# A hybrid RWKV-7 and retention layer on one core: the doubling of the first two units 13 to 15 product groups later, the retention scores two groups later

## The chip, the cores and the metric

The kernel runs on one core of a Trainium2 chip. The metric is the device time of one execution in microseconds (us). Before the change the median of 3 runs is 1264.73 us (1264.21 to 1268.22).

## The reference, cut to what matters

One decoder layer on 256 tokens of width 2048. One input projection feeds two head groups. Group A is RWKV-7 time mixing (16 heads of 64, a state that is updated token by token), group B is retention (4 heads of 256). Their outputs are joined, go through one output projection, a layer norm, a squared-ReLU MLP of width 8192 and a second layer norm.

```python
def _hybrid_layer(x, ...):
    h = x @ w_in                                  # 2048 x 7424
    y_a = _rwkv7_mix(h[..., :RWKV_SHIFT_WIDTH], ...)
    q, k, v, g = jnp.split(h[..., RWKV_SHIFT_WIDTH:], RET_SPLITS, axis=-1)
    y_b = _retention_mix(q, k, v, g, ret_gn_w)
    mix = jnp.concatenate([y_a, y_b], axis=-1) @ w_o
    x = _layer_norm(ALPHA * x + mix, ln1_w, ln1_b)
    ff = jnp.square(jax.nn.relu(x @ w_up)) @ w_down
    return _layer_norm(ALPHA * x + ff, ln2_w, ln2_b)

def step(S, inp):                                 # RWKV-7, one token
    sa = jnp.einsum('bhvk,bhk->bhv', S, a_t)
    S = S * w_t[:, :, None, :] + sa[..., None] * b_t[:, :, None, :] + v_t[..., None] * k_t[:, :, None, :]
    y_t = jnp.einsum('bhvk,bhk->bhv', S, r_t)
```

## The kernel before, in words

**Large products.** All weights arrive as 202 chunks of 1 MB. A chunk comes as two halves `raw` (L138, on SP's queue), ScalarE rounds each half to `whi` (L140) and VectorE takes the rest `wlo = raw - whi` (L141), so that three float32r products stand for one float32 product. `whi` and `wlo` have four buffers each, `raw` three. TensorE then runs the chunk: 48 products of 256 columns in `stat_tile` (L157), or 24 of 512 columns in `mov_chunk` (L173). A quarter of a chunk is a **group**: 12 products of 256 columns, or 6 of 512. After each group the generator yields. The input projection has 58 chunks, so 232 groups.

**Small work between the groups.** `large()` (L506) runs the large products in a fixed order: the low-rank inputs, then for u = 0 to 3 the k, r and v columns of RWKV unit u (4 heads, a quarter of group A), and after each a share of the retention (`RET_SPLIT`). `interleave` (L840) calls, after each group, every live `rwkv_unit(u)` whose count has run down. `yield LAG["x"]` in a unit means: go on after so many groups. One unit runs through these steps:

- the decay and the norm of k (L558 to L617), which end in `kk`, `bt`, `ar` (L624 to L631);
- `gram` (L644): four blocks of 64 x 64 products with `ar`, masked by VectorE (L646);
- the inverse of a unit triangular 32 x 32 block for all heads at once, 31 pairs of a product `prod` (L699) and a sum into `xb` (L701) on VectorE;
- the **round trip**: `xb` goes to DRAM (`dxt`, L708) and comes back as `xc` in another layout (L710), on SP's queue, where the loads of `raw` also stand;
- the second head sum and the bonus (`head_sum`, L583 and L584; L730 to L732), then `xt`, the transposed `xc` (L736), then `yield LAG["bg"]`, which is 4;
- the **doubling**: the inverse of the 64 x 64 block from those of the two 32 x 32 blocks, `d1` (L747) and `d2` (L758) on TensorE with copies `pt` (L751) and `xt` (L763) between;
- the **state steps**, four of them (L770 to L817), each with `f1` (L779, L781), a copy `rhs` by ScalarE (L784), a product (L787), a copy `sa` (L789), `f2` (L795, L796), the new state on VectorE (L803 to L806) and `f3` (L810 to L813); lags of 2, 2 and 1 groups stand between them;
- the head norm and the result into `mxh` and `mxl` (L820 to L838).

The retention counts in groups too: `later(RLAG[0], ...)` (L478) runs the scores of a head (L420, L422) four groups after its rotated `qk` have been set going on POOL (L471, L472), and `later(RLAG[1], ...)` runs `outputs` (L432 to L445) four groups after those. The gate (L487 to L503) reads what `outputs` leaves in `vt`.

**The order on each engine.** The text above is only the program's order. A scheduling layer then lays out each engine's queue: it may put an instruction that it takes to be ready ahead of one that it takes to be still waiting. Within a queue nothing overtakes. So a lag sets where a step may stand, not where it does. Small tiles in PSUM (`sm`) share four banks.

The line that the change replaces, and the two tables:

```python
LAG = dict(..., vtok=8, bg=4, d1=3, d2=1, f1=1, sa=2, st=2, yc=2)   # L81
RLAG = (4, 4)                                                       # L83
            xt = tmp("xt")
            V.transpose(out=xt, in_=xc)
            yield LAG["bg"]                                         # L737
```

Of the kernel before, what the change touches and what calls it, by code (L numbers as in the profile page):

```python
# [77 lines left out]

STRETCH = (78, 106, 138, 170)

LAG = dict(lora=2, scan=3, sq=5, rn=1, kk=7, bt=2, g1=1, btok=1, ktok=2, g2=1, sub=3, xt=2, vtok=8, bg=4, d1=3, d2=1, f1=1, sa=2, st=2, yc=2)  # L81

RLAG = (4, 4)  # L83

SUB_YIELD = (6, 10, 13, 16, 19, 21, 23, 25, 27, 29)
NSHORT = 10
# [15 lines left out]
def tile_hybrid_layer(ctx, tc, xT, xtok, ws, pp, lup, glup, ln1r, ln2r, cst, rope, dmask, eye, out):  # L102
# [14 lines left out]
    def sm_bank():  # L117
        return ps.tile([P, 512], F32, name="sm", tag="sm", bufs=4)
# [115 lines left out]
    def dcol(base, j):  # L234
        return dp[:, base + j:base + j + 1]
# [38 lines left out]
    with ExitStack() as rctx:  # L274
# [7 lines left out]
        def tmp(name, bufs=1, n=512):  # L282
            if name in LONG or n < 256:
                return rp.tile([P, n], F32, name=name, tag=name, bufs=2 if name in TWO else bufs)
            if name in RET:
                return rp.tile([P, n], F32, name=name, tag="rshort", bufs=4)
            return rp.tile([P, n], F32, name=name, tag="short", bufs=NSHORT)
# [112 lines left out]
        def retention():  # L400
# [4 lines left out]
            def later(n, fn):  # L405
                pend.append([n, fn])
# [10 lines left out]
            def scores(h, vt, q, k, dmt):  # L417
                sc = sm_bank()
                for i in range(2):
                    TE.matmul(sc[:, 0:T], k[:, T * i:T * i + P], q[:, hs[i]], start=i == 0, stop=i == 1)  # L420
                for i in range(2):
                    TE.matmul(sc[:, T:T + P], k[:, T * i + P:T * i + T], q[:, T * i + P:T * i + T],  # L422
                              start=i == 0, stop=i == 1)
                pm = tmp("pm", n=384)
                V.tensor_tensor(out=pm[:, 0:T], in0=sc[:, 0:T], in1=dmt, op=ALU.mult)
                V.tensor_tensor(out=pm[:, T:T + P], in0=sc[:, T:T + P], in1=dmt[:, 0:P], op=ALU.mult)
                later(RLAG[1], lambda: outputs(h, vt, pm))

            def outputs(h, vt, pm):
                yb = sm_bank()  # L430
                hv = slice(T * (h % 2), T * (h % 2) + T)
                TE.matmul(yb[:, 0:T], pm[:, 0:P], vt[:, 0, hv], start=True, stop=True)  # L432
                TE.matmul(yb[:, T:2 * T], pm[:, P:T], vt[:, 0, hv], start=True, stop=False)
                TE.matmul(yb[:, T:2 * T], pm[:, T:T + P], vt[:, 1, hv], start=False, stop=True)
                st6 = tmp("st6", n=12)
                mv = tmp("mv", n=4)
                for tt in range(2):
                    V.bn_stats(out=st6[:, 6 * tt:6 * tt + 6], in_=yb[:, hs[tt]])
                    V.bn_aggr(out=mv[:, 2 * tt:2 * tt + 2], in_=st6[:, 6 * tt:6 * tt + 6])
                var = tmp("rvar", n=2)  # L440
                V.tensor_scalar(out=var, in0=mv.rearrange("q (a b) -> q a b", b=2)[:, :, 1], scalar1=RET_EPS,
                                scalar2=None, op0=ALU.add)
                rs = rsqrt(rp, var, 2)
                for tt in range(2):
                    V.tensor_scalar(out=vt[:, tt, hv], in0=yb[:, hs[tt]], scalar1=mv[:, 2 * tt:2 * tt + 1],  # L445
                                    scalar2=rs[:, tt:tt + 1], op0=ALU.subtract, op1=ALU.mult)

            for n in range(2):
# [9 lines left out]
                for h in (2 * n, 2 * n + 1):  # L458
# [18 lines left out]
                    nc.gpsimd.dma_start(out=dmt, in_=dmask[:, T * h:T * h + T])  # L477
                    later(RLAG[0], lambda h=h, vt=vt, qk=qk, dmt=dmt: scores(h, vt, *qk, dmt))  # L478
                    yield "end"
# [43 lines left out]
        def rwkv_unit(u):  # L523
# [16 lines left out]
            def split(src):  # L540
                t = rp.tile([P, 512], F32R, name="lsp", tag="short", bufs=NSHORT)
                hi, lo = t[:, 0:T], t[:, T:2 * T]
                S.copy(hi, src)
                V.tensor_tensor(out=lo, in0=src, in1=hi.bitcast(F32), op=ALU.subtract)
                return hi, lo
# [6 lines left out]
            lus = split(lupt)  # L552
            yield LAG["lora"]
            pw, pa = sm_bank(), sm_bank()
# [3 lines left out]
            for p, j in enumerate(js):  # L558
                S.activation(s[:, hs[p]], pw[:, hs[p]], AF.Tanh, bias=dcol(W0H, j), scale=0.5)
                S.activation(a[:, hs[p]], pa[:, hs[p]], AF.Tanh, bias=dcol(A0H, j), scale=0.5)  # L560
            yield LAG["scan"]
            V.tensor_scalar(out=s, in0=s, scalar1=0.5, scalar2=0.5, op0=ALU.mult, op1=ALU.add)
# [12 lines left out]
            def head_sum(src, lag):  # L575
# [4 lines left out]
                V.tensor_tensor(out=lo, in0=src, in1=hi.bitcast(F32), op=ALU.subtract)  # L580
                yield LAG[lag]
                bank = sm_bank()
# [7 lines left out]
            kkr, sq = tmp("kkr"), tmp("sq")  # L590
            for p, j in enumerate(js):
# [8 lines left out]
                            op0=ALU.mult, op1=ALU.add)  # L600
            yield LAG["rn"]
            S.activation(t, y, AF.Square)
            G.tensor_tensor(out=t, in0=t, in1=v, op=ALU.mult)
            yield LAG["rn"]
            V.scalar_tensor_tensor(out=t, in0=t, scalar=10.0 / 3, in1=t, op0=ALU.subtract, op1=ALU.mult)
            V.scalar_tensor_tensor(out=y, in0=t, scalar=5.0, in1=y, op0=ALU.add, op1=ALU.mult)
            S.activation(t, y, AF.Square)
            yield LAG["rn"]
            V.scalar_tensor_tensor(out=t, in0=t, scalar=9.0 / 64, in1=v, op0=ALU.mult, op1=ALU.mult)
            V.scalar_tensor_tensor(out=y, in0=t, scalar=3.0, in1=y, op0=ALU.subtract, op1=ALU.mult)  # L610
            kk = kkr
# [15 lines left out]
            bt, kt_ = tmp("bt"), tmp("kt")  # L627
# [8 lines left out]
            g1, g2 = tmp("g1", n=1024), tmp("g2", n=1024)  # L636
# [28 lines left out]
            def tok(src, name):  # L665

                t, w = tmp(name), tmp("sw")[:, 0:256].rearrange("q (g x) -> q g x", x=32)
                V.transpose(out=t, in_=src)
                for h in range(2):
                    up, dn = slice(64 * h, 64 * h + 32), slice(64 * h + 32, 64 * h + 64)  # L670
                    if name in TOK_V:
                        V.transpose(out=v8(t)[up, :, 32:64], in_=v8(src)[dn, :, 0:32])
                        V.transpose(out=v8(t)[dn, :, 0:32], in_=v8(src)[up, :, 32:64])
                    else:
                        S.copy(w[dn], v8(t)[up, :, 32:64])
                        S.copy(v8(t)[up, :, 32:64], v8(t)[dn, :, 0:32])
                        S.copy(v8(t)[dn, :, 0:32], w[dn])
                return t
# [7 lines left out]
            btok = tok(bt, "btok")  # L686
# [4 lines left out]
            ktok = tok(kt_, "ktok")  # L691
# [28 lines left out]
            vtok = tok(v, "vtok")  # L720
# [5 lines left out]
            g, gg, bg = tmp("g"), tmp("gg"), tmp("bg")  # L726
# [7 lines left out]
            done["free", "v", u] = True  # L734
            xt = tmp("xt")
            V.transpose(out=xt, in_=xc)  # L736
            yield LAG["bg"]  # L737


            def c32(p, n):  # L740
# [27 lines left out]
            st = None  # L768
            for n in range(4):
# [18 lines left out]
                sa = tmp("sa", n=128)  # L788
# [26 lines left out]
                if n < 3:  # L815
                    st = sn
# [6 lines left out]
            yc, ysq = tmp("yc"), tmp("ysq")  # L823
# [17 lines left out]
        def interleave(main, units):  # L841
# [12 lines left out]
            for e in live:  # L854
                for _ in e[1]:
                    pass

        interleave(large(), [rwkv_unit(u) for u in range(4)])


# [325 lines left out]
```

## Time and profile before

| | value |
|---|---|
| median of 3 runs | 1264.73 us (1264.21 to 1268.22) |
| profiled execution, its own time | 1258.88 us |
| span of that execution | 1257.1 us |
| TensorE busy | 1217.3 us, 97% of the span |
| VectorE busy | 840.7 us, 67% |
| ScalarE busy | 560.3 us, 45% |
| GpSimd busy | 101.6 us, 8% |
| DMA | 229.76 MB, 183 GB/s over the span |
| share of the chain that ended last | TensorE 78%, VectorE 9%, DMA 5%, ScalarE 3% |

TensorE's share counts an instruction from its start to its modelled end, and products overlap in the array, so an engine that is "busy" may still be far from its pace. The pace is read from how many products stand in a stretch. The input projection with the units takes the first 470 us or so; after it come the output projection, the MLP and the two norms.

### The profile page before, as it was taken

How to read it: one execution, taken by the hardware profiler on the slowest of the kernel's cores; microseconds unless marked ns; L12 is line 12 of the kernel's file. 1: busy time of each engine (PE TensorE's matmuls, PEld its weight loads, DVE VectorE, ACT ScalarE, POOL GpSimd, SP SyncE). 2: the span in 40 equal slices, each digit the busy share in tenths (PEclk: the TensorE clock that was granted, in tenths of full speed). 3: DMA queues.
4: the chain of work that ended last, by engine and by line, in shares of the span. 5: the costliest groups of instructions: out<-in, count | busy, mean ns of one | idle time of the engine just before them, and what ended most of it. 6: DMA issues, size and time to landing. Idle time of an engine off the chain costs nothing.

```text
span 1257.1 us, 21910 instructions
## 1 busy us (share of the span) xinstructions
PE 1217.3 (97%) x8952; PEld 1096.0 (87%) x8952; DVE 840.7 (67%) x1319; ACT 560.3 (45%) x723; POOL 101.6 (8%) x89
## 2 busy tenths in 40 slices
PE   7998998999999999989999999999999999999996
PEld 7988997879999778769988899988999888999885
DVE  6888897889879855786554555545555545555566
ACT  5545345355435433464444444443444434444341
POOL 0102121001101100008200000000000000000001
PEclk9999999999999999999999999999999999999998
DMA  8565355346444537655655655555555555556553
GB/s 284 201 190 167 96 181 166 86 139 206 141 140 162 172 111 254 196 169 211 240 200 192 206 191 190 187 199 193 198 195 193 193 193 199 191 190 198 186 200 102
DMA packets 86185, 229.76 MB, mean 183 GB/s; under 512 B 30530, under 2 KB 30658, under 8 KB 85316
## 3 DMA queue, kind: packets, MB, share of 16 engines
q1 hardware_dynamic: 83924, 219.38, 53.4%
q0 software_dynamic: 1440, 7.87, 1.8%
q8 instruction: 70, 1.15, 0.4%
q10 hardware_dynamic: 720, 1.11, 0.3%
q14 instruction: 31, 0.25, 0.1%
HBM read 224.59 MB, written 3.74 MB: 182 GB/s over the span
## 4 chain that ended last, share of the span: by engine, by line
PE 78%; DVE 9%; DMA 5%; ACT 3%; issue 1%; POOL 0%; DVEq 0%; ACTq 0%; SPq 0%
PE mm L157 34%; PE mm L173 34%; DMA raw<-in_ws_dram 4%; PE mm L193 3%; DVE wlo L141 3%; PE sm L644 1%; ACT whi L140 1%; DVE prod L699 1%; DVE xb L701 1%; DMA xc<-dxt 1%; DVE wx L141 1%; PE sm L787 1%; PE sm L779 0%; PE sm L810 0%; ACT wx L140 0%
## 5 line engine op out<-in xcount | busy, mean ns | idle before, releaser
L141 DVE TENSOR_TENSOR wlo<-raw,whi 128x1024 fp32r<-128x1024 f32 x372 | 464.1, 1249 | 315.7 <-ACT whi L140 309.0
L140 ACT CAST whi<-raw 128x1024 fp32r<-128x1024 f32 x372 | 391.2, 1052 | 534.7 <-PE mm L157 217.1
L157 PE MATMUL mm<-x1l,whi 128*128 128x256 f32 x928 | 257.1, 277 | 0.0
L157 PE MATMUL mm<-x1h,whi 128*128 128x256 f32 x928 | 257.1, 277 | 0.0
L157 PE MATMUL mm<-x1h,wlo 128*128 128x256 f32 x928 | 257.1, 277 | 0.0
L157 PE MATMUL mm<-xh,whi 128*128 128x256 f32 x640 | 181.4, 283 | 0.0
L157 PE MATMUL mm<-xl,whi 128*128 128x256 f32 x640 | 178.8, 279 | 0.0
L157 PE MATMUL mm<-xh,wlo 128*128 128x256 f32 x640 | 178.1, 278 | 0.0
L157 PEld LDWEIGHTS mm<-x1l,whi 128*128 128x128 f32 x928 | 175.0, 189 | 0.0
L173 PE MATMUL mm<-whi,ul 128*128 128x512 f32 x448 | 174.3, 389 | 0.0
L173 PE MATMUL mm<-whi,uh 128*128 128x512 f32 x448 | 174.3, 389 | 0.0
L173 PE MATMUL mm<-wlo,uh 128*128 128x512 f32 x448 | 174.3, 389 | 0.0
L157 PEld LDWEIGHTS mm<-x1h,wlo 128*128 128x128 f32 x928 | 174.2, 188 | 0.0
L157 PEld LDWEIGHTS mm<-x1h,whi 128*128 128x128 f32 x928 | 174.2, 188 | 0.0
L157 PEld LDWEIGHTS mm<-xh,whi 128*128 128x128 f32 x640 | 120.8, 189 | 3.2 <-issue 1.0
L157 PEld LDWEIGHTS mm<-xl,whi 128*128 128x128 f32 x640 | 120.7, 189 | 1.1 <-issue 0.2
L157 PEld LDWEIGHTS mm<-xh,wlo 128*128 128x128 f32 x640 | 120.7, 189 | 0.3
L173 PEld LDWEIGHTS mm<-wlo,uh 128*128 128x128 f32 x448 | 84.1, 188 | 17.6
L173 PEld LDWEIGHTS mm<-whi,ul 128*128 128x128 f32 x448 | 84.1, 188 | 17.5
L173 PEld LDWEIGHTS mm<-whi,uh 128*128 128x128 f32 x448 | 84.1, 188 | 17.1
L173 PE MATMUL mm<-whi,xh 128*128 128x512 f32 x128 | 51.9, 406 | 0.0
L1076 POOL TENSOR_TENSOR z<-z,lnr 128x512 f32<-128x512 f32 x3 | 3.9, 1293 | 593.6 <-DVE stats L1064 593.6
(272 smaller groups left out, 1621.6 us busy)
## 6 DMA issues: line engine op xcount, KB each, us to landing
raw<-in_ws_dram SPq DMA_DIRECT2D x400, 512.0 KB, 4.4
first<-in_ws_dram SPq DMA_DIRECT2D x8, 256.0 KB, 7.5
z<-in_xtok_dram POOLq DMA_DIRECT2D x2, 1024.0 KB, 11.3
lnr<-in_ln1r_dram POOLq DMA_DIRECT2D x2, 1024.0 KB, 5.4
lnr<-in_ln2r_dram POOLq DMA_DIRECT2D x2, 1024.0 KB, 11.5
xraw<-in_xT_dram SPq DMA_DIRECT2D x3, 512.0 KB, 8.3
dn<-g SPq DMA_DIRECT2D x8, 128.0 KB, 3.8
xc<-dxt SPq DMA_DIRECT2D x8, 128.0 KB, 3.5
```

Of the source, the lines that this page charges most:

```text
L140: S.copy(hi, raw)
L141: V.tensor_tensor(out=lo, in0=raw, in1=hi.bitcast(F32), op=ALU.subtract)
L157: TE.matmul(dst, w[:, c], a, start=n == 0, stop=n == 3 * KT - 1)
L173: TE.matmul(dsts[tt], a, w[:, c], start=first and k4 == 0 and j == 0, stop=last and k4 == 3 and j == 2)
L193: TE.matmul(dst, a, wt[:, o:o + w], start=kq == 0 and k4 == 0 and i == 0, stop=kq == 3 and k4 == 3 and i == 2)
L644: TE.matmul(bank[r, 128 * n:128 * n + 128], src[r, c64(p, n)], ar[r, o:o + 128], start=True, stop=True)
L699: V.tensor_tensor(out=pv, in0=xbv[0:q, 8 - m:8, s0 + 1:32], in1=blkv[0:q, s0:s0 + 1, s0 + 1:32].broadcast_to([q, m, t]), op=ALU.mult)
L701: V.tensor_reduce(out=xbv[0:q, 8 - m:8, s0], in_=pv, axis=AX.X, op=ALU.add)
L787: both(lambda r, p, cp: TE.matmul(sb[r, cp], xt[r, c64(p, n)], rhs[r, cp], start=True, stop=True))
L1076: G.tensor_tensor(out=z[:, tt, cb(n)], in0=z[:, tt, cb(n)], in1=lnr2[:, 0, cb(n)], op=ALU.mult)
```

## The change

The wait after `xt` no longer has one length for all units. It becomes 19 groups for unit 0, 17 for unit 1, and stays 4 for units 2 and 3. The retention scores come six groups after the rotation instead of four. Nothing is computed in another way.

```diff
-LAG = dict(lora=2, scan=3, sq=5, rn=1, kk=7, bt=2, g1=1, btok=1, ktok=2, g2=1, sub=3, xt=2, vtok=8, bg=4, d1=3, d2=1, f1=1, sa=2, st=2, yc=2)
-
-RLAG = (4, 4)
+LAG = dict(lora=2, scan=3, sq=5, rn=1, kk=7, bt=2, g1=1, btok=1, ktok=2, g2=1, sub=3, xt=2, vtok=8, d1=3, d2=1, f1=1, sa=2, st=2, yc=2)
+
+RLAG = (6, 4)
+
+BGLAG = (19, 17, 4, 4)
...
             V.transpose(out=xt, in_=xc)
-            yield LAG["bg"]
+            yield BGLAG[u]
```

From here on the changed kernel's lines have numbers that are higher by two. The queues as built show what the table does to the order.

**TensorE, the doubling of unit 0 and what follows it.** L747 is `d1`, L758 `d2`, L779 `f1` and L787 the product after it, all of unit 0; L583 and L584 are the first head sum of unit 1 and L157 the large products. Before:

```order
L157 MATMUL mm<-xh,wlo 128x256
L747 MATMUL sm<-xc,g_747 32x32
L583 MATMUL sm<-hi,ones 128x512
L584 MATMUL sm<-lo,ones 128x512
L157 MATMUL mm<-xh,whi 128x256
...
L747 MATMUL sm<-xc,g_747 32x32 x15
...
L758 MATMUL sm<-xt,pt 32x32
L779 MATMUL sm<-vtok,g_748 64x64 x3
...
L787 MATMUL sm<-rhs,xt 64x64
```

Now (L749 is `d1`, L760 `d2`, L781 `f1`, L789 the product after it; L646 is the gram of unit 1):

```order
L749 MATMUL sm<-xc,g_747 32x32 x16
L646 MATMUL sm<-ar,bt 64x128 x8
...
L646 MATMUL sm<-ar,kt 64x128 x8
...
L760 MATMUL sm<-xt,pt 32x32 x16
...
L781 MATMUL sm<-vtok,g_748 64x64 x4
...
L789 MATMUL sm<-rhs,xt 64x64 x4
```

Counted in groups of large products from the start, the first `d1` of unit 0 stood behind 73.0 groups and the other fifteen behind 73.8; now all stand behind 75.0. The head sum of unit 1, which stood behind the first `d1` at 73.0, now stands alone at 62.0. The state steps of unit 0 stood in 74.2 to 82.0 and now stand in 79.0 to 97.0. Unit 1 goes the same way: its `d1` from 117.8 to 121.0, its state steps from 118.9 to 130.0 into 125.0 to 143.0. The state steps of unit 2 stand in 172.0 to 190.0 in both. From its `d1` (168.0) on the queue is as before, save for the scores, two groups later (204 to 206 and 220 to 222 for the last two heads).

**VectorE, the same place.** L141 (now L143) takes the low half of a weight, L699 and L701 (L701 and L703) are the inverse of unit 0, L596 to L612 (L598 to L614) the norm of k in unit 1, L736 (L738) the transposition of `xc` for unit 0. Before:

```order
L701 TENSOR_REDUCE xb<-prod 32x8
L631 TENSOR_TENSOR ar<-r,dc 128x8x64
L141 TENSOR_TENSOR wlo<-raw,whi 128x1024 x3
L596 TENSOR_SCALAR v<-sm 128x512
L736 STREAM_TRANSPOSE xt<-xc 128x512
L597 TENSOR_SCALAR t<-v 128x512
L599 TENSOR_SCALAR y<-t 128x512
L680 TENSOR_TENSOR k<-k,kf 128x512
L763 COPY xt<-sm 32x8x32 x2
L141 TENSOR_TENSOR wlo<-raw,whi 128x1024
```

Now:

```order
L703 TENSOR_REDUCE xb<-prod 32x8
...
L612 SCALAR_TENSOR_TENSOR y<-t,y 128x512
L143 TENSOR_TENSOR wlo<-raw,whi 128x1024
L614 SCALAR_TENSOR_TENSOR kkr<-y,kkr 128x512
L143 TENSOR_TENSOR wlo<-raw,whi 128x1024 x2
L628 TENSOR_TENSOR ar<-kkr,s 128x8x64
L630 TENSOR_TENSOR a<-a,kkr 128x512
L633 TENSOR_TENSOR ar<-r,dc 128x8x64
L631 TENSOR_TENSOR bt<-a,di 128x512
...
L143 TENSOR_TENSOR wlo<-raw,whi 128x1024
L738 STREAM_TRANSPOSE xt<-xc 128x512
```

The norm of k of unit 1 stood behind the transposition of `xc`; now it is mixed into the inverse of unit 0 and done before it. The last sum into `xb` stood behind 33 low halves and now stands behind 31; the transposition stood behind 36 and now stands behind 35.

## Rows read from the trace of the kernel before

**Rows 1.** Page, part 1: span, and busy time of each engine.

```profile
span 1257.1 us, 21910 instructions
PE 1217.3 (97%) x8952; PEld 1096.0 (87%) x8952; DVE 840.7 (67%) x1319; ACT 560.3 (45%) x723; POOL 101.6 (8%) x89
```

**Rows 2.** Busy time in stretches: length, each engine's busy us (count), clock, DMA.

```profile
98.00:118.00 20.00, 19.50 (x167) 19.14 (x168) 19.02 (x40) 11.65 (x16) 2.80 (x3) 1.00 0.52 167
118.00:157.00 39.00, 36.78 (x516) 33.45 (x515) 31.73 (x58) 12.01 (x21) 6.70 (x6) 1.00 0.41 113
211.00:258.00 47.00, 42.82 (x526) 37.52 (x526) 34.36 (x65) 13.25 (x23) 6.55 (x6) 0.93 0.43 125
312.00:366.00 54.00, 54.00 (x652) 49.28 (x652) 41.38 (x72) 21.40 (x34) 6.08 (x6) 1.00 0.48 149
```

**Rows 3.** The same stretches, products of 256 columns (L157) alone: PE, PEld.

```profile
118.00:157.00 39.00, 22.28 (x162) 19.45 (x161) 1.00 0.41 113
211.00:258.00 47.00, 22.40 (x151) 19.41 (x150) 0.93 0.43 125
312.00:366.00 54.00, 34.71 (x274) 32.31 (x274) 1.00 0.48 149
```

**Rows 4.** The same stretches, products of 512 columns (L173) alone.

```profile
118.00:157.00 39.00, 0.00 (x0) 0.00 (x0) 1.00 0.41 113
211.00:258.00 47.00, 5.05 (x21) 3.85 (x22) 0.93 0.43 125
312.00:366.00 54.00, 6.35 (x24) 4.27 (x24) 1.00 0.48 149
```

**Rows 5.** Chain that ended last: start us, length us, what.

```profile
118.49 4.28 DMA dxt<-xb
122.78 2.75 DMA xc<-dxt
...
195.43 16.24 PE mm L157 x144
211.67 6.62 DMA xc<-dxt
...
260.33 5.50 PE mm L173 x24
```

**Rows 6.** Timeline around both round trips: start us, length us, instruction, idle before.

```profile
118.07 0.39 DVE L701 TENSOR_REDUCE xb<-prod 32x8 f32<-32x248 f32 x1
...
125.57 0.24 PE L747 MATMUL sm<-xc,g 32*32 32x32 f32 x2 [2.22 <-DMA xc<-dxt]
...
206.43 0.40 DVE L701 TENSOR_REDUCE xb<-prod 32x8 f32<-32x248 f32 x1
...
213.87 0.28 PE L157 MATMUL mm<-xh,wlo 128*128 128x256 f32 x1
...
218.33 0.31 PE L747 MATMUL sm<-xc,g 32*32 32x32 f32 x2 [4.18 <-DMA xc<-dxt]
...
219.59 0.41 PE L157 MATMUL mm<-xh,whi 128*128 128x256 f32 x1
219.83 0.69 DVE L596 TENSOR_SCALAR v<-sm 128x512 f32<-128x512 f32 x1 [3.62 <-PE sm L584]
```

**Rows 7.** Waits: who waited for whom, us in total, times, longest.

```profile
PE sm L420 <- POOL qk L472: 3.9, 3, 1.9
...
PE sm L493 <- issue: 1.3, 1, 1.3
...
PE sm L583 <- ACT hi L579: 1.4, 1, 1.4
```

**Rows 8.** VectorE by line and form from 98 to 158 us: count, busy us, mean ns.

```profile
L805 DVE TENSOR_TENSOR st<-sm,st 128x64 f32<-128x64 f32 x4 | 0.7, 220 | 0.2
...
L609 DVE SCALAR_TENSOR_TENSOR t<-t,v 128x512 f32<-128x512 f32 x1 | 0.7, 692 | 0.5 <-ACT t L607 0.5
...
L599 DVE TENSOR_SCALAR y<-t 128x512 int32<-128x512 int32 x1 | 0.4, 427 | 0.0
```

**Rows 9.** Page, part 5: the split on VectorE over the whole span.

```profile
L141 DVE TENSOR_TENSOR wlo<-raw,whi 128x1024 fp32r<-128x1024 f32 x372 | 464.1, 1249 | 315.7 <-ACT whi L140 309.0
```

## The prediction

> **What bounds the kernel now.** I read the page's busy shares first, then the busy time by stretch, then the chain and the timeline at the two places where TensorE stands still. TensorE counts as busy for 97% of the span [rows 1], so whatever the change can gain must lie in how slowly it goes while it is "busy". For that the pace has to be known. In the chain 144 products of 256 columns take 16.24 us and 24 of 512 columns 5.50 us [rows 5]: 0.113 and 0.229 us each where nothing disturbs. A group, 12 of the one or 6 of the other, is thus 1.36 to 1.37 us.
>
> The reader should now take three stretches [rows 2] in which the small work is the same: one unit's doubling and state steps, the next unit's gram, one head sum. From 118 to 157 us (unit 0 with the gram of unit 1) there are 162 products of 256 columns [rows 3]: 39.0 - 162 x 0.113 = 20.7 us go to everything else. From 211 to 258 us (unit 1 with the gram of unit 2) there are 151, and 21 of 512 columns [rows 3, 4]: 47.0 - 17.1 - 4.8 = 25.1 us. From 312 to 366 us (unit 2 with the gram of unit 3) there are 274 and 24: 54.0 - 31.0 - 5.5 = 17.5 us. The same small work costs 3.2 us more at unit 0 and 7.6 us more at unit 1 than at unit 2.
>
> The timeline says why. At unit 0 the last sum into `xb` begins at 118.07 us and `d1` starts at 125.57, after 2.22 us in which TensorE stood [rows 6]; between them lie the two transfers, 4.28 and 2.75 us [rows 5]. At unit 1 it is 206.43 to 218.33 us with 4.18 us of standing, and the second transfer alone takes 6.62 us. After that wait a product of 256 columns is shown with 0.41 us [rows 6], and the mean granted clock of the stretch is 0.93 [rows 2]: some 6.6 of the 47 us were at the lower of the two levels, 1.2 GHz. And the state steps, which a lag should set apart, had piled up behind the late `d1`: 8 groups at unit 0 instead of the 18 that they span at unit 2. With few large products between two steps, TensorE waits for each copy.
>
> **The change, part by part.** (a) The doubling. In the order as built `d1` itself moves little (73.8 to 75.0 groups, 117.8 to 121.0). What changes is what stands around it. The head sum of unit 1 no longer stands behind the waiting `d1` but 11 groups earlier, and the state steps spread over 18 groups, step for step as they stand at unit 2 in the kernel before. So I price both places by unit 2: -3.2 and -7.6, together **-10.8 us**. This holds the two standing waits (2.2 + 4.2), the time at the lower clock, and the piled-up steps. The other end is 0, if the same steps wait as long where they now stand.
>
> (b) The scores. TensorE stands for 3.9 us in three waits on POOL's `qk`, the longest 1.9 us [rows 7]. Two groups are 2.7 us, more than any of them. POOL's queue itself moves only at the first head, where a small load slips between the two rotations. I take **-3.0 us**; the ends are -3.9 and 0. `outputs` of the first head of all moves behind 123 groups, but its result is read only by the gate at 144.
>
> (c) VectorE's front. The norm of k of unit 1, some eight instructions with three that follow it, comes forward into the inverse of unit 0: nine at 0.69 and two at 0.4 us [rows 8], 7.0 us of work ahead of four to six splits. There VectorE has no room: 19.02 of 20 us busy from 98 to 118 us [rows 2]. A split is 1.25 us [rows 9] and serves 24 products, 2.7 us of TensorE; with four buffers VectorE may be 4 x 2.7 = 10.8 us ahead. If that lead is full, 7 us fit into it and the cost is 0; if it is empty, the whole 7 us are paid. Just before, TensorE already waited 1.4 us behind a late rounding for a head sum [rows 7], so the lead isn't always there. I take **+3.0 us**, between 0 and 7. The work is paid back from 118 us on, where VectorE is busy for only 31.7 of 39 us.
>
> (d) VectorE's own wait for `xc`. From the last sum into `xb` to `d1` it took 7.5 and 11.9 us [rows 6]. In the new order four splits and some six instructions of 0.7 us lie between that sum and the transposition of `xc`, about 9 us: the transposition comes 0 to 3 us too early. The row shows what such a wait is like: VectorE stood 3.62 us before L596 and did no split meanwhile [rows 6]. The Trainium skill ("TensorE: Matmul & The Clock Gate", section "Architectural detail: the array is 16× 32×32, not 1× 128×128") speaks against the change here: it calls VectorE's queue strict FIFO, so a transposition that waits holds every split behind it. By that rule alone what TensorE no longer waits for would be waited for by VectorE, (d) would be +6.5 and the sum -4.3 us; the 3.62 us agree that such waits happen. By the rows I take +0.5, since the lead of (c) hides part, and another +0.5 for the gate of the first retention half, where TensorE now waits 1.3 us [rows 7] and the head norm of unit 1 now falls into the same groups: **+1.0 us**, between 0 and 6.
>
> What costs nothing: unit 0 ends some 15 groups later, and its result is read by the second half of unit 1, which moves by only 3 groups, and by the output projection, behind 232. From `d1` of unit 2 the queues are as before. If that cover were gone, the last unit's tail would follow the last large product and every step would be bare; the order shows that it isn't. The later scores of the last head leave 6 groups, 8 us, between its `outputs` (now 226) and the gate (232).
>
> Sum: -10.8 - 3.0 + 3.0 + 1.0 = **-9.8 us**. The profiled execution took 1258.88 us around a span of 1257.1, so it would take 1249.1; it lies 5.9 us below the median of the runs. I put the same difference on the median: 1264.73 - 9.8 = **1255 us**. The best ends of all terms give -14.7, and with the late head sum of 1.4 and the gate's 1.3 us gone as well -17.4: 1247 us.
>
> **The rivals.** *The wait moves to VectorE.* The transposition waits for `xc` by 3 us at each unit, splits come late, and (c) costs its 3: -10.8 - 3.0 + 3.0 + 6.0 + 0.5 = -4.3, 1260.4 us. For it: the in-order wait of 3.62 us [rows 6] and the round trip of 11.9 us at unit 1. Against it: at unit 0 it was 7.5 us, less than the work between.
>
> *The piling is not what costs.* If the steps wait as long wherever they stand, because VectorE and ScalarE are full with the inverse of unit 1, which now runs beside the state steps of unit 0, only the two standing waits go: -6.4, and +4.0 from (c) and (d), with no gain from the scores: -2.4, 1262.3 us. At unit 2 no inverse ran beside the steps; VectorE was busy for 41.4 of 54 us there [rows 2]. That is what this rival has for it. This is also the case in which the change doesn't do what it says.
>
> *VectorE becomes the bound: slower.* If VectorE enters the front without a lead, (c) costs 7, and then each of the three new states of units 0 and 1 (four instructions of 0.2 us [rows 8]) is found behind one split and two inverse steps, 1.25 + 0.8 = 2 us, while `f1` stands two groups on in TensorE's queue: 6 x 2 = 12. Then -10.8 - 3.0 + 7 + 12 = +5.2, 1269.9 us. It decides where the lead, 10.8 us at most, is used up before the state steps begin. Against it: over the four stretches together VectorE is busy for 126.5 of 160 us [rows 2], so a lead that is lost comes back.
>
> **How the numbers follow.** My forecast has 0.66, the first rival 0.16, the second 0.10, the third 0.08. A measurement of this kernel tells about 0.3%, 3.8 us, from no change. The forecast's own range, -17 to -5, is wholly beyond that; the first rival lies at its edge and counts half; the second is within it. Faster 0.74, same 0.18, slower 0.08. The range from 1246 to 1263 us holds the forecast, the first rival and the middle of the second.
>
> **What would show it.** Right: no wait of TensorE for `xc` over 0.5 us; no stretch at the lower clock near unit 1; the same account (stretch minus products at their pace) near 17.5 us over each of the two new stretches of state steps; the wait of L420 on POOL below 1 us. Wrong: VectorE's transposition of `xc` idle for 3 us or more, or large products that wait for `wlo` between 98 and 150 us, or new waits of L781 for the state on VectorE.

## The result, and the profile after

The changed kernel takes 1248.97 us in the median of 4 runs (1243.16 to 1252.39) against 1264.47 us for the kernel before, measured beside it (1263.71 to 1268.22, 4 runs): a ratio of 0.989, 95% interval 0.985 to 0.9936, some 15.5 us faster. Its profiled execution took 1243.16 us around a span of 1241.4; that of before took 1258.88.

The first two lines of its page, and the shares by engine of the chain that ended last (the page's fourth part):

```profile
span 1241.4 us, 21909 instructions
...
PE 1209.7 (97%) x8952; PEld 1089.2 (88%) x8952; DVE 845.8 (68%) x1319; ACT 559.8 (45%) x723; POOL 102.7 (8%) x89
...
PE 85%; DVE 5%; ACT 2%; DMA 2%; issue 1%; POOL 0%; DVEq 0%; SPq 0%; ACTq 0%
```

TensorE's busy share is 97% as before [rows 1], which by itself tells nothing. The chain does: TensorE's share of it rose from 78% to 85%, and VectorE and DMA, 9% and 5% before, fell to 5% and 2%. What the chain no longer holds is seen in TensorE's waits from 50 to 480 us (us in total, times, longest):

```profile
PE sm L585 <- ACT hi L581: 3.2, 2, 2.0
PE sm L646 <- DVE bt L631: 1.7, 2, 1.4
PE sm L646 <- DVE kt L683: 1.0, 1, 1.0
PE mm L175 <- DVE mxl L840: 0.5, 1, 0.5
PE mm L159 <- DVE wlo L143: 0.5, 1, 0.5
PE sm L495 <- DVE gth L492: 0.4, 1, 0.4
PE sm L586 <- DVE lo L582: 0.2, 1, 0.2
```

The waits for `xc`, 2.2 and 4.2 us [rows 6], are gone, and so are the three on POOL's `qk`, 3.9 us [rows 7]; the gate's 1.3 us fell to 0.4. The same view of the kernel before has these two lines:

```profile
PE sm L583 <- ACT hi L579: 2.6, 2, 1.4
PE sm L644 <- DVE bt L629: 0.4, 1, 0.4
```

So the gram's waits for `bt` and `kt` grew from 0.4 to 2.7 us, and those of the head sums for `hi` from 2.6 to 3.2. Both are for results of the front of VectorE and ScalarE, which now holds more. A wait of 0.5 us of a large product for `wlo` is new as well.

Three stretches of the changed kernel in which the doubling and the state steps of units 0, 1 and 2 stand, first all work, then the products of 256 columns (L159), then those of 512 (L175); columns as in [rows 2]:

```profile
125.00:178.00 53.00, 52.02 (x650) 48.19 (x649) 49.22 (x115) 18.29 (x27) 7.93 (x8) 1.00 0.55 165
216.00:269.00 53.00, 51.56 (x549) 42.30 (x547) 50.37 (x147) 15.91 (x25) 2.98 (x3) 1.00 0.44 133
303.00:357.00 54.00, 54.00 (x653) 49.30 (x652) 42.81 (x74) 22.14 (x36) 6.46 (x6) 1.00 0.49 149
...
125.00:178.00 53.00, 37.45 (x290) 34.29 (x289) 1.00 0.55 165
216.00:269.00 53.00, 11.32 (x87) 10.12 (x85) 1.00 0.44 133
303.00:357.00 54.00, 34.71 (x275) 32.32 (x274) 1.00 0.49 149
...
125.00:178.00 53.00, 0.00 (x0) 0.00 (x0) 1.00 0.55 165
216.00:269.00 53.00, 23.50 (x90) 16.20 (x90) 1.00 0.44 133
303.00:357.00 54.00, 6.35 (x24) 4.28 (x24) 1.00 0.49 149
```

The granted clock is 1.00 in all three, where unit 1 of before had 0.93 [rows 2]. The account (stretch less products at 0.113 and 0.229 us) is 53 - 32.8 = 20.2 us at unit 0, 53 - 9.8 - 20.6 = 22.6 at unit 1 and 54 - 31.1 - 5.5 = 17.4 at unit 2. The first two now hold small work that the third doesn't: eight score products at unit 0, eight and twelve output products at unit 1. The trace prices them: from the first start of such a set to the start of the product behind it the eight take 1.3 us at unit 0 and 1.2 at unit 1, and the outputs 1.5 and 1.2 us, the first of these here:

```profile
222.56 0.70 PE L434 MATMUL sm<-vt,pm 128*128 128x256 f32 x2
...
224.06 1.09 PE L646 MATMUL sm<-ar,bt 64*64 64x128 f32 x16
```

Less these 1.3 and 3.9 us, and less the gram's waits of 1.0 and 1.4 us that lie there, 17.9 and 17.2 us remain, beside 17.4 at unit 2, whose stretch alone holds a head sum (0.5 us).

VectorE at the two transpositions of `xc` (start us, length us, instruction, and in brackets the idle time before it, if any):

```profile
117.78 0.39 DVE L703 TENSOR_REDUCE xb<-prod 32x8 f32<-32x248 f32 x1
...
127.27 0.48 DVE L245 SCALAR_TENSOR_TENSOR v<-mm,ppt,v 128x255 f32<-128x255 f32 x1 [1.69 <-ACT v L244]
127.67 1.22 DVE L143 TENSOR_TENSOR wlo<-raw,whi 128x1024 fp32r<-128x1024 f32 x1
128.80 0.71 DVE L738 STREAM_TRANSPOSE xt<-xc 128x512 f32<-128x512 f32 x1
...
188.43 0.40 DVE L703 TENSOR_REDUCE xb<-prod 32x8 f32<-32x248 f32 x1
...
198.40 0.68 DVE L732 TENSOR_TENSOR bg<-sm,v 128x512 f32<-128x512 f32 x1
199.00 0.70 DVE L738 STREAM_TRANSPOSE xt<-xc 128x512 f32<-128x512 f32 x1
```

There are 11.0 and 10.6 us from the start of the last sum into `xb` to the transposition, and it doesn't wait for `xc` at either unit. That is the sum of two effects: other work lies between, and a transfer into `xc` lands 4.3 to 5.2 us after its issue here.

**Where the time came from.** The table gives the time at which TensorE reached the large group of that number, counted from 1 (12 products of 256 columns or 6 of 512), as the difference to the profiled execution of before. "Again" is a second profile of the changed kernel; "before 2" and "before 3" are two more of the kernel before (all three from the experiments below).

```
group            56     72    104    160    248    384    end
after          -0.4   +1.1   -3.9   -9.2  -11.4  -15.6  -15.7
again          +1.5   +2.7   -2.5   -7.8   -9.8  -10.8  -11.0
before 2       +0.3   +0.3   +5.4   +4.1   +4.1   +4.2   +4.4
before 3       -0.2   -0.2   +1.2   -0.4   -0.5   -2.5   -2.8
```

Stretch by stretch the two profiles of the change agree: +1.5 and +1.2 us in the front (groups 56 to 72), -5.0 and -5.2 at unit 0 with the first head's scores (72 to 104), -5.3 and -5.3 at unit 1 with its gate (104 to 160), -2.2 and -2.0 at the last two heads' scores (160 to 248). From 56 to 248 that makes -11.0 and -11.3. Some work has only moved between these stretches. In the kernel before, unit 1's first head sum and the outputs of the first head stand at unit 0:

```profile
125.75 0.50 PE L583 MATMUL sm<-hi,ones 128*128 128x512 f32 x1
...
178.58 0.59 PE L432 MATMUL sm<-vt,pm 128*128 128x256 f32 x2
```

They take 0.6 and 1.1 us there, to the start of the product behind them; now the head sum stands in the front and the outputs at unit 1 (222.56 us). Behind group 248, where no queue is changed, the two profiles differ (-4.3 and -1.2), and so do two executions of before (-2.3): nothing shows that part to be the change's.

### The profile page after: what moved, and what is told of

The parts are those of the page before. It is cut to its first block, busy times and chain, and to the rows that moved or that the text cites. A ratio compares the mean times of both kernels' runs of the same rounds, so it can differ in the third digit from the quotient of the medians.

```text
span 1241.4 us, 21909 instructions
## 1 busy us (share of the span) xinstructions
PE 1209.7 (97%) x8952; PEld 1089.2 (88%) x8952; DVE 845.8 (68%) x1319; ACT 559.8 (45%) x723; POOL 102.7 (8%) x89
## 4 chain that ended last, share of the span: by engine, by line
PE 85%; DVE 5%; ACT 2%; DMA 2%; issue 1%; POOL 0%; DVEq 0%; SPq 0%; ACTq 0%
PE mm L159 39%; PE mm L175 37%; PE mm L195 4%; DVE wlo L143 1%; DMA raw<-in_ws_dram 1%; PE sm L646 1%; ACT whi L142 1%; PE sm L789 1%; PE sm L781 0%; PE sm L812 0%; DVE wx L143 0%; PE sm L797 0%; PE sm L552 0%; DMA dxt<-xb 0%; PE sm L815 0%
## 5 line engine op out<-in xcount | busy, mean ns | idle before, releaser
L143 DVE TENSOR_TENSOR wlo<-raw,whi 128x1024 fp32r<-128x1024 f32 x372 | 464.8, 1252 | 304.4 <-ACT whi L142 296.9
L159 PE MATMUL mm<-x1l,whi 128*128 128x256 f32 x928 | 256.2, 276 | 0.0
L159 PE MATMUL mm<-x1h,whi 128*128 128x256 f32 x928 | 256.1, 276 | 0.0
L159 PE MATMUL mm<-x1h,wlo 128*128 128x256 f32 x928 | 256.1, 276 | 0.0
L159 PE MATMUL mm<-xh,whi 128*128 128x256 f32 x640 | 181.4, 284 | 0.0
L159 PE MATMUL mm<-xh,wlo 128*128 128x256 f32 x640 | 177.5, 277 | 0.5 <-DVE wlo L143 0.5
L159 PE MATMUL mm<-xl,whi 128*128 128x256 f32 x640 | 177.4, 277 | 0.0
L175 PE MATMUL mm<-whi,ul 128*128 128x512 f32 x448 | 174.3, 389 | 0.0
L175 PE MATMUL mm<-whi,uh 128*128 128x512 f32 x448 | 174.3, 389 | 0.0
L175 PE MATMUL mm<-wlo,uh 128*128 128x512 f32 x448 | 174.3, 389 | 0.0
L159 PEld LDWEIGHTS mm<-x1h,wlo 128*128 128x128 f32 x928 | 174.2, 188 | 0.0
L159 PEld LDWEIGHTS mm<-x1h,whi 128*128 128x128 f32 x928 | 174.2, 188 | 0.0
L159 PEld LDWEIGHTS mm<-x1l,whi 128*128 128x128 f32 x928 | 174.2, 188 | 0.0
L159 PEld LDWEIGHTS mm<-xh,whi 128*128 128x128 f32 x640 | 120.2, 188 | 3.6 <-issue 1.4
L159 PEld LDWEIGHTS mm<-xh,wlo 128*128 128x128 f32 x640 | 120.3, 188 | 1.0 <-DVE wlo L143 0.7
L159 PEld LDWEIGHTS mm<-xl,whi 128*128 128x128 f32 x640 | 120.4, 188 | 0.3
L175 PEld LDWEIGHTS mm<-wlo,uh 128*128 128x128 f32 x448 | 84.1, 188 | 17.6
L175 PEld LDWEIGHTS mm<-whi,uh 128*128 128x128 f32 x448 | 84.1, 188 | 17.4
L175 PEld LDWEIGHTS mm<-whi,ul 128*128 128x128 f32 x448 | 84.1, 188 | 17.2
L175 PE MATMUL mm<-whi,xh 128*128 128x512 f32 x128 | 52.7, 412 | 0.0
```

The lines of the kernel that those rows point to most:

```text
L143: V.tensor_tensor(out=lo, in0=raw, in1=hi.bitcast(F32), op=ALU.subtract)
L159: TE.matmul(dst, w[:, c], a, start=n == 0, stop=n == 3 * KT - 1)
L175: TE.matmul(dsts[tt], a, w[:, c], start=first and k4 == 0 and j == 0, stop=last and k4 == 3 and j == 2)
```

## The experiments

Where no other base is named, the edits are made to the changed kernel: `BGLAG` holds the lags of the doubling for the four units, `RLAG` those of the scores and the outputs. The kernel before took 1265.56 us (median of 27 runs) beside the first four kernels.

**The doubling alone.**

```diff
-RLAG = (6, 4)
+RLAG = (4, 4)
```

> Only the doubling's lags (19, 17, 4, 4); the scores stay at 4 groups. Theory (the two terms add): the doubling brings 9 to 10 us of the 13.5, so 1254 to 1256 where before is 1264.5; TensorE waits for POOL's qk at L420 as before, 3 to 4 us in three waits, and not for xc. Rival (the scores' lag is what frees PSUM banks and the queues around unit 1, the doubling alone brings little): 1260 or more.

Measured: 1252.83 us (1249.71 to 1256.91, 9 runs), ratio 0.9918 [0.9887, 0.9949], a little better than the theory's 1254 to 1256. No wait for `xc` is left, and of the scores' waits two:

```profile
PE sm L422 <- POOL qk L474: 2.3, 2, 1.9
```

**The scores alone.** This edit is made to the kernel before.

```diff
-RLAG = (4, 4)
+RLAG = (6, 4)
```

> Only the scores two groups later; the doubling stays at 4. Theory: the three waits of L420 for POOL go (3.9 us), part of it comes back at the gate: 1261 to 1263 where before is 1264.5, and d1 still waits for xc by 2 us at unit 0 and 4 us at unit 1. Rival (scores and doubling help one another): no gain alone, 1264 to 1265.

Measured: 1256.19 us (1251.33 to 1262.08, 12 runs), ratio 0.993 [0.9899, 0.996], faster than both expectations. Here TensorE's waits are the mirror image, none for POOL and both for `xc`:

```profile
PE sm L747 <- DMA xc<-dxt: 5.8, 2, 2.9
```

The two medians are 12.7 and 9.4 us below before, together 22.1, more than the 16 or 17 of both at once. The medians do not add; the mean granted clock, which the results list for each execution, says why. On that chip the 27 executions of before had 0.978 to 0.996 (median 0.988), the doubling alone 0.994 to 0.997, the scores alone 0.985 to 0.995. Among executions at 0.994 or more the means are 1256.9 us for before (5), 1252.8 for the doubling (9), 1253.1 for the scores (5): -4.2 and -3.8 before rounding. The changed kernel has 0.994 to 0.997 in all 10 of its executions, here and in the run again, and 1248.0 us in the mean; the nine such executions of before among the 65 beside the experiments have 1256.2. That is -8.2 for both, and the parts sum to -7.9. One wait is in both parts: at the first head's scores the kernel before waits 1.6 us for POOL, and the doubling alone takes that away too. So some 2 us of the whole are not in the parts, about what means of five to ten executions can tell (those five of before lie between 1254.1 and 1259.4).

**Unit 0 alone.**

```diff
-RLAG = (6, 4)
+RLAG = (4, 4)
...
-BGLAG = (19, 17, 4, 4)
+BGLAG = (19, 4, 4, 4)
```

> Only unit 0's doubling later (19, 4, 4, 4), scores at 4. Theory (each unit's round trip is a loss by itself, 3.2 us at unit 0 and 7.6 at unit 1 by the account): 3 to 4 us faster than before, 1260.5 to 1261.5, with the wait of d1 for xc at unit 1 still there, and the clock's fall with it if the wait stays over 4 us. Rival (unit 1's loss follows from unit 0's lateness and heals with it): 8 us or more faster, no wait for xc at unit 1.

Measured: 1252.38 us (1248.76 to 1256.37, 7 runs), ratio 0.9907 [0.9872, 0.9942]: all that the doubling gave at both units. No wait for `xc` is left at unit 1 either. The order as built shows how: with unit 0's steps spread, unit 1's `d1` stands behind 108.5 groups instead of 117.8 and its state steps spread over 114 to 130 by themselves. The rival of this expectation was right: unit 1's loss was in good part a consequence of unit 0's.

**Unit 1 alone.** The same, with `BGLAG = (4, 17, 4, 4)`.

> Only unit 1's doubling later (4, 17, 4, 4), scores at 4. Theory: 5.5 to 7.5 us faster than before, 1257 to 1259; unit 0's d1 waits 2 us for xc as before, unit 1's not, and the clock stays at its upper level. Rival (the loss at unit 1 is the pile of steps that unit 0 leaves behind): under 3 us faster.

Measured: 1253.09 us (1251.03 to 1261.74, 12 runs), ratio 0.9926 [0.9899, 0.9953]. The wait at unit 0 stays, and behind it this execution ran long at the lower clock; the stretch of unit 0, and the wait in it:

```profile
118.00:157.00 39.00, 36.72 (x416) 32.78 (x415) 22.61 (x44) 9.48 (x17) 4.79 (x4) 0.74 0.27 83
...
PE sm L749 <- DMA xc<-dxt: 2.3, 1, 2.3
```

A clock of 0.74 over 39 us is 20 us at the lower of the two levels (0.26 x 39 x 2). The median gain of 12.5 us is above the 5.5 to 7.5 of the theory, and the rival's under 3 fails too. Beside unit 0 alone it tells that either unit's lag gives some 12 to 13 us in the median and the second little more; why unit 1's lag alone is worth so much while unit 0's loss stays, no run tells.

**`d1` early, the wait behind it.** The kernel before took 1265.14 us (27 runs) beside this kernel and the next three. The doubling begins after 4 groups as before, and the 15 and 13 groups stand between `d1` and `d2`; scores after 4.

```diff
-RLAG = (6, 4)
+RLAG = (4, 4)
...
-BGLAG = (19, 17, 4, 4)
+BGLAG = (4, 4, 4, 4)
...
-            yield LAG["d1"]
+            yield LAG["d1"] + (15, 13, 0, 0)[u]
```

> d1 stays where it stood before (behind 73.0 and 116.0 groups, with the head sum behind it, so TensorE still stands for xc), but 15 and 13 groups more lie between d1 and d2, so that the state steps are spread over 81 to 97 and 125 to 143 groups; scores at 4. Theory A (the time goes in the pile of small steps, where TensorE has so few large products that the clock falls): granted clock of 0.994 or more in nearly all executions, median 1252 to 1256 where before is 1265. Theory B (the standing wait for xc makes the clock fall and is most of the loss): clocks of 0.983 to 0.990 in most executions as before, 1261 or more.

Measured: 1256.22 us (1253.65 to 1260.82, 12 runs), ratio 0.9957 [0.9929, 0.9984], clock 0.990 to 0.995, between what the two theories expected. One wait for `xc` of 2.5 us stays, and the gram now waits 3.2 us for `bt`. So spreading the steps gives part of the doubling's gain; the rest needs `d1` late as well. Which of the wait for `xc`, the gram's wait and the lower clock behind each of them keeps it back here isn't shown.

**Late, but piled.** The whole change, with no lags between `d1`, `d2`, `f1`, `sa` and `st` of units 0 and 1 (one such line; the other four go alike):

```diff
+PACED = ()
...
-            yield LAG["d1"]
+            if u > 1 or "d1" in PACED: yield LAG["d1"]
```

> The change, but without the lags between d1, d2 and the state steps of units 0 and 1: no wait for xc, and the steps piled into 75 to 79 and 121 to 125 groups, denser than before. Theory A: the clock falls again in most executions (mean granted clock 0.990 or less), median 1258 to 1266. Theory B: no wait, no fall: clock 0.994 or more, median within 4 us of the change, 1249 to 1253.

Measured: 1260.25 us (1255.78 to 1265.71, 12 runs), ratio 0.9982 [0.9954, 1.001], clock 0.989 to 0.995, 12 us more than the change beside it. `d1` comes as late as in the change and no wait for `xc` is left; TensorE waits elsewhere:

```profile
PE sm L587 <- ACT hi L583: 6.2, 2, 5.4
PE sm L762 <- ACT pt L755: 2.3, 2, 1.8
```

The longest of these waits doesn't stand at a pile. The first head sum of unit 2 stands behind 104.0 groups here, as in the kernel before, and behind 108.25 in the change. There it waits 2.0 us; here it waits 5.4 and the lower clock follows, 0.94 in the mean over the stretch where the change has 1.00:

```profile
197.66 0.80 PE L587 MATMUL sm<-hi,ones 128*128 128x512 f32 x1 [5.37 <-ACT hi L583]
...
157.00:211.00 54.00, 48.53 (x392) 47.32 (x389) 49.10 (x121) 26.41 (x42) 11.90 (x12) 0.94 0.45 139
```

Set beside the profile of the change again, as in the table, this one loses 3.2 us from group 72 to 104, 5.8 from there to 120, where that head sum stands, and 5.2 from there to 160. So some 8 of these 14 us are at the two piles. Steps that follow each other with few large products between cost about that much, even without a wait for `xc`; what the two waits alone are worth, this kernel doesn't show, since it has another wait in their place.

**The change again.**

> The change itself, beside the two others: 1247 to 1251, granted clock 0.994 or more in all executions (theory A and B alike).

Measured: 1247.96 us (1245.91 to 1250.04, 6 runs), ratio 0.9883 [0.9845, 0.9921], clock 0.994 to 0.997.

**Unit 3 sooner.** The last unit's steps are still piled, in 235 to 239 groups. Its last head sum comes after one group instead of eight, so that `d1` stands behind 224 groups and the steps in 228 to 238.

```diff
-            bo = yield from head_sum(k, "vtok")
+            bo = yield from head_sum(k, "vtok" if u < 3 else "rn")
```

> The change, and unit 3's last head sum 1 group after its split instead of 8: its d1 stands behind 224 instead of 231 groups, its state steps in 228 to 238 instead of 235 to 238. Theory A: the last pile, some 3 us of waits and slow steps around groups 232 to 240, shrinks: 2 to 3 us faster than the change, 1245 to 1248. Theory B: no wait for xc stood there, so nothing changes, or 1 us is lost in a new wait of the head sum.

Measured: 1254.25 us (1251.94 to 1257.26, 10 runs), ratio 0.9922 [0.9894, 0.9949], 6.3 us more than the change: a miss, and a useful one, for it brings back at unit 3 what the change took away at units 0 and 1. The wait, and the stretch after it:

```profile
PE sm L749 <- DMA xc<-dxt: 3.9, 1, 3.9
...
413.00:424.00 11.00, 10.73 (x73) 8.00 (x75) 2.55 (x11) 1.16 (x3) 0.00 (x0) 0.56 0.33 100
```

**Unit 0 and the scores.** The kernel before took 1263.16 us (11 runs) beside this one and the next.

```diff
-BGLAG = (19, 17, 4, 4)
+BGLAG = (19, 4, 4, 4)
```

> The doubling wait is 19 groups for unit 0 alone and the scores' lag is 6; unit 1 keeps 4. Theory (unit 1's loss followed from unit 0's lateness, so unit 1's own lag does nothing further): the time of the change, 1246 to 1251 us, no wait of TensorE for xc at unit 1 and none for POOL at the scores, mean granted clock 0.994 or more in most runs. Rival (the two lags add): unit 1's wait and its piled steps stay, some 3 to 5 us above the change, 1251 to 1254 us, with a wait for xc of over 1 us between 170 and 260 us.

Measured: 1249.14 us (1244.74 to 1251.75, 6 runs), ratio 0.9886 [0.9862, 0.991], the change's own 0.9883 within its interval; clock 0.993 to 0.997. There is no wait for `xc` and none for POOL. The theory holds: the entry for unit 1 can be left at 4. Its profile has 6.8 us at the lower clock at 199 to 206 us, which neither profile of the change has, and the gate's wait of 1.3 us is back; the interval leaves room for the microsecond or two that these are worth.

**Unit 3's inverse sooner.** Another way to spread unit 3's steps, 227 to 237 groups, without a wait for `xc`.

```diff
-BGLAG = (19, 17, 4, 4)
+BGLAG = (19, 17, 4, 6)
...
-                    yield LAG["sub"]
+                    yield LAG["sub"] - (u == 3)
```

> The change, with unit 3's inverse one group shorter in each of its steps (lag 2 instead of 3) and its doubling wait 6 instead of 4, so that its state steps stand in 227 to 237 groups. Theory (what is left to gain is the last unit's piled steps, as long as its d1 does not wait for xc): 2 to 3 us below the change, 1244 to 1247 us, and no wait for xc over 0.5 us at unit 3. Rival (VectorE cannot do the inverse faster than its lags allow, so TensorE waits at the inverse or for xc as it did when a head sum was brought forward): slower than the change by 2 to 6 us, with a wait for xc or for the inverse's data of 1 to 4 us after 380 us.

Measured: 1251.02 us (1248.83 to 1253.75, 6 runs), ratio 0.9899 [0.9876, 0.9923]: not faster than the change. No wait for `xc` came, but one of 2.0 us for POOL's `qk`, and 3.4 us at the lower clock at 408 us. Neither theory named that wait; the rival's time is the nearer.

**The kernel before, two more profiles.**

> The kernel before, unchanged, for another profile of it. Theory (most executions of before lose time to falls of the granted clock at the two piled stretches, which the profiled execution on record mostly escaped): if its mean granted clock is below 0.992, the profile shows two or more stretches at half clock between 115 and 260 us, of 3 to 20 us each, and the time is 1261 to 1270 us. Rival (the executions differ in waits on transfers): the time is that high with one clock fall of 7 us or none, and the wait for xc is over 6.4 us in all.

> The same kernel a third time. The same two theories: stretches at half clock add to about half their length over the 1257 us of an execution without them; or longer waits for transfers at equal clock.

Measured: 1263.29 us with a mean clock of 0.992, and 1256.05 us with 0.994; an execution beside them that has no profile took 1269.22 us with 0.983. In the first, TensorE's wait for `xc`, then stretches around both units:

```profile
PE sm L747 <- DMA xc<-dxt: 6.4, 2, 3.4
...
118.00:127.30 9.30, 6.29 (x54) 6.00 (x54) 5.22 (x7) 2.46 (x3) 3.40 (x3) 1.00 0.67 201
127.30:137.50 10.20, 10.20 (x109) 8.94 (x108) 5.30 (x9) 2.83 (x6) 1.27 (x1) 0.51 0.27 88
137.50:157.00 19.50, 19.50 (x295) 17.61 (x296) 15.53 (x34) 4.80 (x10) 0.00 (x0) 0.99 0.14 36
...
211.00:258.00 47.00, 43.64 (x537) 39.31 (x536) 35.84 (x63) 15.80 (x26) 5.67 (x6) 0.96 0.50 138
```

In the second:

```profile
118.00:157.00 39.00, 36.84 (x501) 33.48 (x501) 29.94 (x55) 11.58 (x21) 5.42 (x6) 0.96 0.38 104
211.00:258.00 47.00, 43.76 (x538) 38.52 (x537) 35.17 (x66) 13.90 (x23) 6.69 (x6) 0.96 0.48 130
```

In the first the waits for `xc` add up to what they were, 6.4 us, so the rival falls. TensorE stood 3.0 us at unit 0 and then ran for 10.2 us at 1.2 GHz (0.51), with 109 products in them; the table shows this execution 5.4 us later at group 104 than the one on record, which ran its unit 0 at 1.00. The Trainium skill ("TensorE: Matmul & The Clock Gate", section "Terms") puts the price of throttled time at that time multiplied by the share of the clock that is missing, here a half. The trace agrees within a microsecond: 5.1 us by it and 0.8 us of longer wait make 5.9, against 5.4. In the second each unit has a clock of 0.96, about 3.4 us at the lower level. Between the start and the last microseconds the lower clock thus stands only at the two piled stretches in the three profiles of before, each time right behind a wait for `xc`, and its length changes from execution to execution: none, 10.2 and 3.4 us at unit 0, 6.8, 3.4 and 3.4 at unit 1.

## Why the prediction was right, and where it was off

The direction and the range held, and the likeliest case was the one that came; the time was 6 us too high (1255 for 1249).

**(a) The doubling, -10.8.** At unit 0 the stretch gave -5.0. But one of the three waits on POOL lay there, 1.6 us, and 0.6 and 1.1 us are the head sum and the outputs that only moved away: -1.7 is left for the -3.2. At unit 1 it gave -5.3, with those outputs (1.5 us there) come in and the gate's wait 0.9 us shorter: -5.9 for -7.6. The account after is 17.9 and 17.2 us, near the 17.5 of unit 2, so the steps themselves did come to unit 2's price. What the term left out are the gram's new waits, 1.0 and 1.4 us, which stand there as well, and that unit 0's price held a head sum that is moved and not saved. That the two units are separate terms was wrong, as unit 0 alone showed.

**(b) The scores, -3.0.** All three waits went, the end that I gave as -3.9; alone and at equal clock the edit was worth 3.8 us, though the doubling would have taken 1.6 us of it by itself.

**(c) VectorE's front, +3.0.** It cost 1.2 to 1.5 us by group 72, and about half of that is the head sum that now stands there. The lead hid more than I took.

**(d) VectorE's wait and the gate, +1.0.** There is no such wait, and the gate's fell by 0.9 us instead of growing. The rule that VectorE's queue is strict FIFO ("TensorE: Matmul & The Clock Gate", section "Architectural detail: the array is 16× 32×32, not 1× 128×128", of the Trainium skill) isn't contradicted by it: `xc` had landed when its transposition came up, so the queue had nothing to hold.

That the sum came near is in part luck: (a) was 3 us too good, (c) and (d) together some 3 to 4 us too dear.

**The step that failed** is the last: "I put the same difference on the median". The sum, -9.8, stands against -11.0 and -11.3 over the groups that the change touches, and against -8.2 between executions at a granted clock of 0.994 or more. The medians differ by 15 to 17 us. The profiled execution of before had a clock of 0.995, and most runs have less: a median of 0.988 is 0.007 x 1265 = 9 us of clock short of it. The change takes away what those runs lose too, and none of that was in the sum. (These clocks are of the 27 runs beside the experiments; for the four beside the result none is on record.) The clock stood in my account, as 6.6 us in one execution, but as something fixed.

The rivals: no wait moved to VectorE. *The piling is not what costs* is refuted by the late, piled kernel: there the waits for `xc` are gone, the time is nearly that of before, and some 8 of the 14 us that its profile loses are at the two piles. VectorE was not the bound; its busy 49 and 50 us of 53 at units 0 and 1 show that it wasn't far from it.

Of the signs listed, four came as written (no wait for `xc`, no lower clock near unit 1, none for POOL, none at the transposition) and the account came within half a microsecond, the gram's waits counted apart. Of the signs against, one came at a small size: a large product waits 0.5 us for `wlo` at 120 us. New waits stand at the gram, 2.7 us, not at L781.

Open: what part of the median's gain the scores owe to the clock. They leave both waits for `xc`, and yet the median clock rose from 0.988 to 0.991; no run tells why. Open too is how the gain of the doubling divides between the waits and the piles: in both kernels that keep one without the other, a further wait came in.

## What to carry to other kernels

Read the granted clock of the profiled execution beside that of the timed runs before a sum is carried from one to the other: with 0.995 against 0.988, the profile hid about half of what a change was worth. A chain of small dependent steps is to be set apart by lags, not only begun when its data is there: late but piled, the steps gave back some 8 us of the gain. And one lag may heal the next stage too, so try the first one alone before setting both.

## What was not expected of the hardware

The same kernel on one core runs at a mean granted clock between 0.978 and 0.997, and its time follows: 1252.6 us at 0.997, 1269.3 at 0.982, with the order of every queue fixed. TensorE stays at the lower clock in stretches in which the profile shows it busy without a gap, 10.20 of 10.20 us. What stands before is a wait: apart from the first and the last microseconds the fourteen profiles have 22 such falls, and 21 of them follow right behind a wait of TensorE of 1.8 to 5.4 us, ten of them a wait for `xc` and six one for `hi`. The other one, of 3.4 us, stands in the pile of unit 0 of the late, piled kernel. The four longest, 10.2 to 20.5 us, each follow a wait for `xc` of 2.3 to 3.9 us. But the wait doesn't settle it: that of 2.0 us for `hi` at 195 us or so has no fall behind it in the two profiles of the change, 3.4 us with unit 3 sooner and 6.8 us with unit 0 and the scores. At unit 3 a single wait of 3.9 us, put back where the change has none, came with 0.56 over the 11 us after it, and that kernel is 6.3 us slower than the change in the median.
